# Two-layer trunk (S5 mixer, dilated attention, conv-GLU): the low part of the keys kept per head in both row halves, so that both products of a score tile use 128 rows

## The chip, the cores and the metric

One core of one Trainium2 chip runs the whole program. The metric is the device time of the program in microseconds (us), the median of its runs. The engines are TensorE (PE, with its weight loads as PEld), VectorE (DVE), ScalarE (ACT), GpSimd (POOL) and SyncE (SP), which issues nearly all DMAs.

## The reference

A trunk of two layers over 1024 tokens of 1024 features, fp32. Layer 0 mixes with a state-space model (S5), layer 1 with attention; each is followed by a conv-GLU feed-forward, with layer norms around. Cut to the attention, in which the change lies:

```python
kv = h @ w_kv                                 # keys and values: 3 groups x 16 heads x 64
q = (h @ w_q) * 64 ** -0.5
for g, dil in ((0, 1), (1, 4), (2, 16)):      # nearest group, two dilated groups
    # residue blocks of 128 tokens with step dil; a block sees itself and the one before it
    s = einsum('brnqhe,brnkhe->brnhqk', qb, kb) + bias[g]      # scores, 64 features per head
    s = where(valid, s, -1e30)
    lse = logsumexp(s); p = exp(s - lse)
    o_g = einsum('brnhqk,brnkhe->brnqhe', p, vb)
w = softmax(stack(lse over the 3 groups))     # the groups merged by their weights
out = sum_g w_g * o_g  ->  @ w_out
```

## The kernel before, in words

**Precision.** A product of two fp32 matrices is made of parts: a tensor is split into a high part (rounded to fp32r) and a low part (the rest, in fp32r). `mm3` (L86 to L90) gives three products: high x high, high x low, low x high.

**Stages.** S5 (to about 205 us), its gate and output projection, the first feed-forward, values of all heads (`value_tile`, to DRAM as `vscr`), then from about 1400 to 2440 us the attention by pairs of heads, then its output projection and the second feed-forward. The products outside the attention are not touched.

**A pair of heads** (`Pair`, eight pairs). For each of three groups `proj` (L407) makes queries and keys of both heads, 128 features x 1024 tokens: per tensor two halves of 512 tokens, each 24 products (tile qk, L88 to L90). ScalarE brings a half from PSUM to tile qt (L430 for queries, L432 for keys) and writes its high part (L436); for keys it writes it a second time (L438). GpSimd subtracts to get the low part (L441).

The layout decides which products can be made. X is one tile per head (named qs in the profile, for queries and keys alike), 128 rows: head 0 has its 64 features in rows 0 to 63, head 1 in rows 64 to 127. Queries: the high part in the head's own 64 rows, the low part in the other 64. Keys: the high part in both halves. The low part of the keys stands in kl, one tile for both heads, each head in its own 64 rows.

A score tile takes two products into the same PSUM region (`smm`, L481): L488 over 128 rows (query high and low, by key high in both halves) and L489 over the head's 64 rows (query high by key low). Their weights are the queries (128 columns); the keys move, 256 or 128 columns. Score tiles: per head 7 of 256 and 1 of 128 columns in the nearest group, 4 and 4 in each dilated group, so 384 in all, 240 of 256 columns and 144 of 128. Two or four of them share a PSUM buffer (tile s, four buffers, shared with the transposes).

VectorE adds the bias and takes the maximum in one instruction per score tile (L477), into p. ScalarE makes the exponentials (L508, L534). `softmax` (L540) merges the statistics and scales p (L557, L564) on VectorE. `output` (L584) loads V of the three groups (L589, tile V, three buffers), transposes p on TensorE (tile t, L605), brings it to SBUF (L608) and multiplies with V (tile o, L615); first the nearest group, then both dilated ones into a second PSUM tile.

**What orders the work.** A scheduler puts each engine's instructions into a fixed order at build time; an engine then runs its list in order and waits where an operand or a buffer isn't there. Projections run about a group ahead of scores: the queries and keys of the next group or the next pair are made between the scores of this one, and serve to fill TensorE's time during the softmax. Buffers bound how far: pool `ap` (`setup`, L669) has eight buffers for q (X and kl, five to a group), two for qt, three for V. So the last tiles of a group's keys wait until the scores of the group before have read theirs. SP has one queue: a load that waits for a buffer holds up those behind it.

Of the kernel before, what the change touches and what calls it, by code (L numbers as in the profile page):

```python
# [9 lines left out]
F32 = mybir.dt.float32  # L10
F32R = mybir.dt.float32r
# [7 lines left out]
P = 128  # L19
# [9 lines left out]
class Pool:  # L29
    """a tile pool with a fixed number of buffers for every tag"""  # L30
# [9 lines left out]
class Net:  # L40
# [55 lines left out]
    def type1(self, ps, w, xT, halves=(0, 1)):  # L96
        """ps[P, 1024] = w^T x, w = (hi, lo) as [P, KT, 128]"""
# [39 lines left out]
    def ln_final(self, acc, gb, tt):  # L137
        """with gain and bias: ((x - mean) gain) r + bias"""
# [21 lines left out]
    def to_T(self, accs, hf, li, xp, tmp):  # L160
        """transposes four normalized token tiles; gain and bias; split. -> list of KT tiles"""
# [20 lines left out]
    def ffn(self, l, accs, hT, xp, wd_pool, first_half, after):  # L182
        """first_half(): called when the products that need only the first half of hT are out"""
# [71 lines left out]
        for i in range(nch):  # L255
            c = list(range(i * CH, i * CH + CH))
            aT = [up(f) for f in c]
            if i == nch - 1:
                # the transposed input is no longer needed: its buffers take the last weights
# [10 lines left out]
def bias_onehot():  # L270
    """[64, 3, 384] selectors: row b picks rel_bias[b], row 32 the mask; column j is distance 255 - j"""
# [24 lines left out]
def attn_bias_rows(net, pool, ps1):  # L296
    """rel_bias by distance, one row for each head -> DRAM"""
# [16 lines left out]
def attn_bias(net):  # L314
    """a copy of the rows for each query row, to be read skewed"""
# [7 lines left out]
def skew(scr, h0, q0, qstep, nq):  # L323
    """[nq, 2 heads, 256] view: element (q, k) = row[127 - q + k], q = q0 + qstep * i"""
# [5 lines left out]
def tok_cols(xh, g, j):  # L330
    """columns of key tile j of layout g in a token half tile [P, 512]"""
    if g == 0:
        q = (j % 4) * P
        return slice(q, q + P)
    return slice(j // 2, 512, 4)
# [6 lines left out]
def value_tile(net, blk, j, hT, ws, ps, st):  # L342
    """values of four heads for a key tile: token-major, per group in its key order, kept in DRAM"""
# [12 lines left out]
def values_first(net, hT, pool):  # L356
    """the value tiles that need only the first half of the tokens, before the second half is there"""
# [9 lines left out]
def attention(net, hT, ap, ws):  # L367
# [25 lines left out]
    # the buffers of hT take the output  # L393
# [13 lines left out]
def proj(net, w, hT, g, isq, ap):  # L407
# [3 lines left out]
    # per head, rows of 64: queries (hi, lo), keys (hi, hi); the second head has its halves swapped  # L411
    X = [ap.tile([P, T], F32R, "q", "qs") for _ in range(2)]
    kl = None if isq else ap.tile([P, T], F32R, "q", "kl")
    for hf in range(2):
# [18 lines left out]
        for h in range(2):  # L433
# [5 lines left out]
            lo = X[h][o, sl] if isq else kl[r, sl]  # L439
# [997 lines left out]
```

## Time and profile before

| | us |
|---|---|
| runs | 3305.84, 3303.48, 3299.15 |
| median | 3303.48 |
| span of the profiled execution, first to last instruction | 3296.0 |
| around the span, taken as median less span | 7.5 |
| TensorE busy | 3128.0 (95%) |
| VectorE busy | 1745.0 (53%) |
| ScalarE busy | 1072.5 (33%) |
| GpSimd busy | 589.8 (18%) |
| mean granted clock of TensorE, share of full | 0.952 |

The device time of the profiled execution itself isn't given beside its span, so the span is set against the median of the runs. How to read the rows: a timeline row has start, duration, engine, line, operation, tiles as out<-in, operand shape and count; in brackets the idle time ahead of it and what ended it. Matmuls are pipelined, so the duration of one is longer than what it keeps the engine from the next; the step from start to start shows that. In a row of grouped instructions stand count, busy time, mean ns of one, idle time ahead. PEclk is the share of full clock that TensorE was granted.

### The profile page before, as it was taken

The page shows a single profiled execution, that of the slowest core. Times are in us where ns is not written, and L with a number is a line of the kernel's source. Part 1 is how long each engine was busy: PE and PEld are TensorE (multiplying, and loading weights), DVE is VectorE, ACT ScalarE, POOL GpSimd, SP SyncE. Part 2 cuts the span into 40 slices and gives each one's busy share as a digit, 9 for nine tenths or more (in the row PEclk, how much of TensorE's full clock was granted, in tenths as well). Part 3 has the DMA queues.
Part 4 walks back from the last instruction along what each step waited for, and adds up shares of the span by engine and source line. Part 5 has one row for each costly group of instructions (what it writes and reads, how often), then busy time and mean ns, then how long its engine had stood idle before and what let it go on. Part 6 is the DMA issues. An engine that isn't in the chain of part 4 may idle for free.

```text
span 3296.0 us, 36786 instructions
## 1 busy us (share of the span) xinstructions
PE 3128.0 (95%) x14422; PEld 2524.8 (77%) x14422; DVE 1745.0 (53%) x3348; ACT 1072.5 (33%) x1868; POOL 589.8 (18%) x447
## 2 busy tenths in 40 slices
PE   4789999999999999999999999999969999999997
PEld 3668878888888789977767777777747788888886
DVE  8954764455444621135455455355457755454447
ACT  2433332222222311145444445454433322222222
POOL 8910140000000000022222222222343500000001
PEclk8889999999999999999989998998979999999999
DMA  5232321111111243211111111111134111111121
GB/s 172 65 117 77 122 64 45 52 52 45 45 52 50 92 125 99 90 36 48 55 51 43 43 58 37 51 61 36 52 127 135 64 52 43 54 50 47 45 64 51
DMA packets 98413, 219.63 MB, mean 67 GB/s; under 512 B 9664, under 2 KB 51248, under 8 KB 98240
## 3 DMA queue, kind: packets, MB, share of 16 engines
q1 hardware_dynamic: 96128, 207.85, 19.9%
q0 software_dynamic: 2112, 9.44, 0.9%
q8 instruction: 113, 1.85, 0.2%
q14 instruction: 60, 0.49, 0.0%
HBM read 191.49 MB, written 35.20 MB: 69 GB/s over the span
## 4 chain that ended last, share of the span: by engine, by line
PE 84%; DVE 8%; POOL 4%; ACT 2%; issue 1%; DMA 1%; SPq 0%; ACTq 0%; POOLq 0%; DVEq 0%
PE dn L236 14%; PE up L89 10%; PE up L88 10%; PE up L90 10%; PE qk L88 5%; PE qk L90 4%; PE qk L89 4%; PE s L489 4%; PE s L488 3%; PE v L88 3%; PE v L90 3%; PE v L89 3%; PE o L615 2%; DVE p L564 2%; PE t L605 2%; PE wo L88 2%
## 5 line engine op out<-in xcount | busy, mean ns | idle before, releaser
L84 DVE TENSOR_TENSOR wl<-raw,wh 128x1024 fp32r<-128x1024 f32 x261 | 337.6, 1295 | 739.0 <-ACT wh L83 738.4
L83 ACT CAST wh<-raw 128x1024 fp32r<-128x1024 f32 x261 | 274.0, 1051 | 1104.0 <-PE up L89 473.2
L88 PE MATMUL up<-hT,wh 128*128 128x512 f32 x1408 | 549.4, 391 | 12.1 <-DVE u L212 12.1
L89 PE MATMUL up<-hT,wh 128*128 128x512 f32 x1408 | 549.6, 391 | 1.0 <-DVE hT L84 1.0
L90 PE MATMUL up<-hT,wl 128*128 128x512 f32 x1408 | 549.3, 391 | 0.0
L441 POOL TENSOR_TENSOR qs<-qt,qs 64x512 fp32r<-64x512 f32 x96 | 125.8, 1311 | 1290.6 <-ACT qs L436 1246.6
L88 PE MATMUL qk<-hT,wh 128*128 128x512 f32 x768 | 328.6, 428 | 0.0
L89 PE MATMUL qk<-hT,wh 128*128 128x512 f32 x768 | 322.7, 420 | 0.0
L90 PE MATMUL qk<-hT,wl 128*128 128x512 f32 x768 | 322.6, 420 | 0.0
L88 PEld LDWEIGHTS up<-hT,wh 128*128 128x128 f32 x1408 | 265.3, 189 | 67.7 <-issue 12.9
L89 PEld LDWEIGHTS up<-hT,wh 128*128 128x128 f32 x1408 | 265.6, 189 | 57.4 <-DVE hT L84 2.3
L90 PEld LDWEIGHTS up<-hT,wl 128*128 128x128 f32 x1408 | 265.5, 189 | 55.2
L212 DVE SCALAR_TENSOR_TENSOR u<-up,cw,u 128x1022 f32<-128x1022 f32 (+1 forms) x176 | 224.6, 1278 | 30.4 <-ACT u L208 28.2
L477 DVE CUSTOM_DVE_ANT_0 p<-s,bt 128x256 f32<-128x256 f32 (+1 forms) x384 | 125.6, 372 | 211.8 <-PE s L489 211.1
L246 DVE TENSOR_TENSOR acc<-acc,dn 128x1024 f32<-128x1024 f32 x144 | 174.9, 1217 | 92.1 <-PE dn L236 90.0
L236 PE MATMUL dn<-wh,ah 128*128 128x512 f32 x704 | 216.8, 389 | 0.0
L236 PE MATMUL dn<-wl,ah 128*128 128x512 f32 x704 | 216.7, 389 | 0.0
L236 PE MATMUL dn<-wh,al 128*128 128x512 f32 x704 | 216.6, 389 | 0.0
L441 POOL TENSOR_TENSOR kl<-qt,qs 64x512 fp32r<-64x512 f32 x96 | 123.6, 1293 | 391.5 <-PE s L488 261.3
L88 PEld LDWEIGHTS qk<-hT,wh 128*128 128x128 f32 x768 | 156.2, 203 | 38.8 <-issue 4.7
L90 PEld LDWEIGHTS qk<-hT,wl 128*128 128x128 f32 x768 | 156.4, 204 | 34.5
L89 PEld LDWEIGHTS qk<-hT,wh 128*128 128x128 f32 x768 | 156.7, 204 | 32.9 <-issue 0.7
(248 smaller groups left out, 5096.6 us busy)
## 6 DMA issues: line engine op xcount, KB each, us to landing
raw<-in_w_up SPq DMA_DIRECT2D x88, 512.0 KB, 3.5
raw<-in_w_out SPq DMA_DIRECT2D x48, 512.0 KB, 3.5
raw<-in_w_down SPq DMA_DIRECT2D x44, 512.0 KB, 3.5
raw<-in_w_v SPq DMA_DIRECT2D x25, 512.0 KB, 3.5
vscr<-vs SPq DMA_DIRECT2D x48, 256.0 KB, 2.3
V<-vscr SPq DMA_DIRECT2D x24, 512.0 KB, 4.1
raw<-in_w_q SPq DMA_DIRECT2D x24, 512.0 KB, 3.5
raw<-in_w_k SPq DMA_DIRECT2D x24, 512.0 KB, 3.6
```

What stands on the lines that cost most here:

```text
L83: nc.scalar.copy(hi, x)
L84: (eng or nc.vector).tensor_tensor(out=lo, in0=x, in1=hi.bitcast(F32), op=ALU.subtract)
L88: nc.tensor.matmul(out, lh, rh, start=first, stop=False)
L89: nc.tensor.matmul(out, lh, rl, start=False, stop=False)
L90: nc.tensor.matmul(out, ll, rh, start=False, stop=last)
L212: nc.vector.scalar_tensor_tensor(out=tf[:, d:], in0=ps[:, : T - d], scalar=cw[:, d, ft : ft + 1], in1=tf[:, d:], op0=ALU.mult, op1=ALU.add,)
L236: nc.tensor.matmul(ps[:, h * 512 : h * 512 + 512], l_, w[wi][:, h * 512 : h * 512 + 512], start=(i == 0 and l_ is ah and wi == 0), stop=(i ...
L246: nc.vector.tensor_tensor(out=accs[tt][:], in0=accs[tt][:], in1=ps[:], op=ALU.add)
L441: e.tensor_tensor(out=lo, in0=tmp[r], in1=hi.bitcast(F32), op=ALU.subtract)
L477: nc.vector.tensor_tensor_reduce(out=out, in0=s, in1=b, scale=1.0, scalar=-3.0e38, op0=ALU.add, op1=ALU.max, accum_out=m)
L488: nc.tensor.matmul(out, qx[:, qs], kv[0], start=True, stop=False)
L489: nc.tensor.matmul(out, qx[r, qs], kv[1], start=False, stop=True)
```

## The change

The low part of the keys, kl, becomes one tile per head like X, and GpSimd writes it into both halves of the 128 rows: twice the operations for kl. The second product of a score tile then takes all 128 rows of the queries (high and low) by key low in both halves; that adds the product low x low, which was left out. Both products stand on one line now. Of the attention's buffers q gets nine instead of eight (six tiles to a group now), V two instead of three. In the changed file comments and docstrings are gone, and lines from here on have numbers one or two smaller (L440 for L441, L488 for both L488 and L489, L588 for L589).

```diff
@@ proj
     X = [ap.tile([P, T], F32R, "q", "qs") for _ in range(2)]
-    kl = None if isq else ap.tile([P, T], F32R, "q", "kl")
+    kl = None if isq else [ap.tile([P, T], F32R, "q", "kl") for _ in range(2)]
...
             if not isq:
                 nc.scalar.copy(X[h][o, sl], tmp[r])
-            lo = X[h][o, sl] if isq else kl[r, sl]
-            e = nc.gpsimd
-            e.tensor_tensor(out=lo, in0=tmp[r], in1=hi.bitcast(F32), op=ALU.subtract)
+            for lo in [X[h][o, sl]] if isq else [kl[h][r, sl], kl[h][o, sl]]:
+                nc.gpsimd.tensor_tensor(out=lo, in0=tmp[r], in1=hi.bitcast(F32), op=ALU.subtract)
@@ smm
-            r = slice(64 * h, 64 * h + 64)
-            qx, kx, kl = q[0][h], k[0][h], k[1]
+            qx, kv = q[0][h], [k[0][h][:], k[1][h][:]]
             if isinstance(ks, int):
-                kv = [x.rearrange("p (n r q) -> p n r q", n=2, r=4)[:, :, ks, :] for x in (kx[:], kl[r])]
+                kv = [x.rearrange("p (n r q) -> p n r q", n=2, r=4)[:, :, ks, :] for x in kv]
             else:
-                kv = [kx[:, ks], kl[r, ks]]
-            nc.tensor.matmul(out, qx[:, qs], kv[0], start=True, stop=False)
-            nc.tensor.matmul(out, qx[r, qs], kv[1], start=False, stop=True)
+                kv = [x[:, ks] for x in kv]
+            for i in range(2):
+                nc.tensor.matmul(out, qx[:, qs], kv[i], start=(i == 0), stop=(i == 1))
@@ setup
-    return net.pool("ap", ctx, q=8, qt=2, V=3, oT=1, p1=2, p4=2, bt=1, pt=4)
+    return net.pool("ap", ctx, q=9, qt=2, V=2, oT=1, p1=2, p4=2, bt=1, pt=4)
```

The scheduler makes a new order from this. TensorE, in the second pair, at the first score tile of head 1 in the nearest group (s is the score tile, qs the keys' and the queries' X, kl the low part of the keys, qk a projection). Before, the products alternate between lines and rows, and after one tile projections follow:

```order
L488 MATMUL s_10271<-qs_9780,qs_9710 128x128
L489 MATMUL s_10271<-kl_9781,qs_9710 128x128
L488 MATMUL s_10271<-qs_9780,qs_9710 128x256
L489 MATMUL s_10271<-kl_9781,qs_9710 128x256
L88 MATMUL qk_10516<-hT_7472,wh_10510 128x512
L89 MATMUL qk_10516<-hT_7472,wh_10510 128x512
L90 MATMUL qk_10516<-hT_7472,wl_10511 128x512
```

The same place of TensorE's list afterwards:

```order
L88 MATMUL qk_10572<-hT_7656,wh_10535 128x512
L89 MATMUL qk_10572<-hT_7656,wh_10535 128x512
L488 MATMUL s_10291<-qs_9795,qs_9725 128x128
L488 MATMUL s_10291<-kl_9797,qs_9725 128x128
L488 MATMUL s_10291<-qs_9795,qs_9725 128x256
L488 MATMUL s_10291<-kl_9797,qs_9725 128x256
L488 MATMUL s_10298<-qs_9795,qs_9725 128x256
L488 MATMUL s_10298<-kl_9797,qs_9725 128x256
```

The tile stood ahead of 20 projection products and stands behind 21 of them now, with the three other tiles of its head right after it. GpSimd, at the keys of the second group of the same pair (kl, qt and qs as above). Before:

```order
L441 TENSOR_TENSOR kl_10387<-qt_10413,qs_10385 64x512
L441 TENSOR_TENSOR kl_10387<-qt_10446,qs_10385 64x512
L441 TENSOR_TENSOR kl_10387<-qt_10413,qs_10386 64x512
L441 TENSOR_TENSOR kl_10387<-qt_10446,qs_10386 64x512
L441 TENSOR_TENSOR qs_10514<-qt_10541,qs_10514 64x512
L441 TENSOR_TENSOR qs_10515<-qt_10541,qs_10515 64x512
```

The same place of GpSimd's list afterwards:

```order
L440 TENSOR_TENSOR kl_10407<-qt_10434,qs_10405 64x512 x2
L440 TENSOR_TENSOR kl_10407<-qt_10469,qs_10405 64x512 x2
L440 TENSOR_TENSOR kl_10408<-qt_10434,qs_10406 64x512 x2
L440 TENSOR_TENSOR kl_10408<-qt_10469,qs_10406 64x512 x2
L440 TENSOR_TENSOR qs_10539<-qt_10566,qs_10539 64x512
L440 TENSOR_TENSOR qs_10540<-qt_10566,qs_10540 64x512
```

The order is the same, both halves of head 0 first, with every kl operation doubled and the queries' low parts behind eight operations instead of four. SP, at the end of the first pair's output (V is a V load, raw a weight load, oscr the store of the output). Before, all three loads there are for the second pair:

```order
L589 DMA V_10859<-vscr 128x1024
L75 DMA raw_11320<-in_w_q 128x1024
L589 DMA V_10861<-vscr 128x1024
L589 DMA V_10863<-vscr 128x1024
L666 DMA oscr<-oT_10105 128x1024
```

The same place of SP's list afterwards:

```order
L588 DMA V_9872<-vscr 128x1024
L75 DMA raw_11355<-in_w_q 128x1024
L588 DMA V_10894<-vscr 128x1024
L588 DMA V_10896<-vscr 128x1024
L665 DMA oscr<-oT_10125 128x1024
```

The first load there is now the first pair's own third one, which the products of its last group read soon after; the second pair's third load has moved to the same place a pair later.

## Prediction

> **What bounds the kernel now.** I read the page first (busy shares, then the chain that ended last), then TensorE's timeline in the attention stage, then windows for the granted clock.
>
> ```profile
> span 3296.0 us, 36786 instructions
> ...
> PE 3128.0 (95%) x14422; PEld 2524.8 (77%) x14422; DVE 1745.0 (53%) x3348; ACT 1072.5 (33%) x1868; POOL 589.8 (18%) x447
> ...
> PE 84%; DVE 8%; POOL 4%; ACT 2%; issue 1%; DMA 1%; SPq 0%; ACTq 0%; POOLq 0%; DVEq 0%
> PE dn L236 14%; PE up L89 10%; PE up L88 10%; PE up L90 10%; PE qk L88 5%; PE qk L90 4%; PE qk L89 4%; PE s L489 4%; PE s L488 3%; PE v L88 3%; PE v L90 3%; PE v L89 3%; PE o L615 2%; DVE p L564 2%; PE t L605 2%; PE wo L88 2%
> ```
>
> TensorE (PE; PEld is its weight load) is busy in 95% of the span and carries 84% of the chain, the score products (tile s) 7%; DVE comes next with 53% busy. So a microsecond saved on PE counts, as long as no wait takes its place. The change works in the attention stage, about 1400 to 2400 us, on the two products that make a score tile: L488 over 128 rows, L489 over 64. Two stretches of PE's timeline (start, duration, ...):
>
> ```profile
> 1700.51 0.38 PE L488 MATMUL s<-qs,qs 128*128 128x256 f32 x1
> 1700.82 0.38 PE L489 MATMUL s<-kl,qs 64*128 64x256 f32 x1
> 1701.13 0.39 PE L488 MATMUL s<-qs,qs 128*128 128x256 f32 x1
> ...
> 1716.38 0.32 PE L489 MATMUL s<-kl,qs 64*128 64x128 f32 x1
> 1716.64 0.33 PE L488 MATMUL s<-qs,qs 128*128 128x128 f32 x1
> 1716.90 0.32 PE L489 MATMUL s<-kl,qs 64*128 64x128 f32 x1
> ```
>
> Products overlap, so the cost of one is the step from its start to the next start: 0.31 us with 256 columns, 0.26 with 128. Halving the columns saves only 0.05; about 0.2 us of each step does not depend on them. Compare stretches in which the rows do not change:
>
> ```profile
> 1755.48 0.39 PE L88 MATMUL qk<-hT,wh 128*128 128x512 f32 x1
> 1755.71 0.39 PE L89 MATMUL qk<-hT,wh 128*128 128x512 f32 x1
> ...
> 1756.16 0.46 PE L488 MATMUL s<-qs,qs 128*128 128x256 f32 x3
> 1756.55 0.38 PE L489 MATMUL s<-kl,qs 64*128 64x128 f32 x2
> ...
> 1554.01 1.53 PE L605 MATMUL t<-ident,p 128*128 128x128 f32 x12
> 1555.29 0.48 PE L88 MATMUL qk<-hT,wh 128*128 128x512 f32 x1
> ```
>
> A projection product of 512 columns steps at 0.23, less than an L489 of 256. Three L488 that the order happens to put in a row take 0.39 to the next start, 0.13 each, the change to 64 rows at their end included. Twelve transposes, each 128x128 with weights of its own, take 1.28, so 0.107 each. The 0.2 us is the price of the change between 128 and 64 rows, paid at every score product.
>
> **The change part by part.**
>
> (1) The score products. Counts, by form:
>
> ```profile
> L489 PE MATMUL s<-kl,qs 64*128 64x256 f32 x240 | 96.3, 412 | 0.0
> ...
> L488 PE MATMUL s<-qs,qs 128*128 128x256 f32 x240 | 92.9, 394 | 0.7 <-DVE mg L477 0.5 <-ACT qs L438 0.2
> ...
> L489 PE MATMUL s<-kl,qs 64*128 64x128 f32 x144 | 52.6, 365 | 0.0
> L488 PE MATMUL s<-qs,qs 128*128 128x128 f32 x144 | 48.8, 339 | 0.0
> ```
>
> At full clock they cost 480 x 0.31 + 288 x 0.26 = 224 us today. Afterwards all 768 use 128 rows. For 256 columns I take 0.12 (the row of three, less the change at its end), for 128 columns 0.11 (the transposes): 480 x 0.12 + 288 x 0.11 = 89 us. Gain 135. Bounds: no gain if the 0.2 us belongs to something else; 224 - 768 x 0.107 = 142 if every step falls to the transposes'.
>
> The weight load of one product:
>
> ```profile
> 1755.48 0.19 PEld L89 LDWEIGHTS qk<-hT,wh 128*128 128x128 f32 x1
> ```
>
> It runs beside the product ahead of it (0.39 long, step 0.23), and all rows there are in use. The Trainium skill ("TensorE: Matmul & The Clock Gate", Part 3, The mechanism) says otherwise: a weight load overlaps a running product only where the row groups differ. By that rule the change would put every load behind its product; the row speaks against it, and rival B prices it.
>
> (2) The granted clock. One window over the stage, then four of 4 us from one pair (busy times by engine, then PEclk, DMA share, GB/s):
>
> ```profile
> 1400.00:2400.00 1000.00, 980.59 (x4335) 722.04 (x4333) 510.21 (x1875) 473.85 (x1066) 261.92 (x202) 0.91 0.15 48
> ...
> 1552.00:1556.00 4.00, 4.00 (x37) 3.40 (x36) 1.12 (x2) 2.47 (x3) 0.00 (x0) 1.00 0.22 70
> ...
> 1576.00:1580.00 4.00, 4.00 (x17) 2.37 (x14) 2.77 (x9) 0.00 (x0) 0.00 (x0) 1.00 0.70 206
> 1580.00:1584.00 4.00, 4.00 (x11) 2.94 (x11) 1.81 (x9) 3.72 (x9) 3.91 (x4) 0.62 0.52 187
> ...
> 1592.00:1596.00 4.00, 4.00 (x10) 3.00 (x11) 3.78 (x17) 0.20 (x1) 2.23 (x2) 0.50 0.01 2
> ```
>
> 0.91 over 1000 us is 90 us lost. The clock falls to half right behind runs of scores, although PE counts as busy in all of the 4 us: with a step of 0.31, of which half a 512-column step (0.11) is work, the array is two thirds empty. Afterwards a run of 16 such products lasts 1.9 us instead of 5, nearly filled, with projections around it. I take three quarters of the 90 back, 68 us; bounds 0 and 90. The Trainium skill (same page, Part 1) has the gate at half or full rate by activity in windows of about 3.4 us; whether it counts these short products as activity no row here shows, which is rival C.
>
> (3) GpSimd (POOL). Each key tensor's low part is now written twice per half and head, 8 operations instead of 4.
>
> ```profile
> 1580.02 5.09 POOL L441 TENSOR_TENSOR kl<-qt,qs 64x512 fp32r<-64x512 f32 x4 [37.22 <-PE s L488]
> ...
> L441 POOL TENSOR_TENSOR kl<-qt,qs 64x512 fp32r<-64x512 f32 x96 | 123.6, 1293 | 391.5 <-PE s L488 261.3 <-issue 62.3 <-ACT qs L436 58.9
> ...
> L441 POOL TENSOR_TENSOR qs<-qt,qs x96: 1258/1277/1552, 1410.7 to 2371.4; 64x512 fp32r<-64x512 f32 x96
> ```
>
> That is 96 x 1.29 = 124 us more, on an engine with 262 of these 1000 us busy. It costs time only where PE waits. The tightest place: the keys of the next group wait for head 0's last score (the row at 1580.02), then take 8 x 1.29 = 10.3 us instead of 5.1. In the new order PE has between that score and the next group's first second product 31 projection products (7.1 us) and 16 scores (1.9): 9.0 us, and needs the first two operations only (2.6 us). Head 1's keys, ready after 10.3, are asked for 3 to 5 us later still. The query parts queued behind on POOL (5.2 us) are asked for after some 26 us. No cost; if POOL were late by all eight, 1.3 us a group, 31 us in all.
>
> (4) VectorE's (DVE's) reductions free the four PSUM buffers of the scores.
>
> ```profile
> 1578.94 0.42 DVE L477 CUSTOM_DVE_ANT_0 p<-s,bt 128x256 f32<-128x256 f32 x1 [0.48 <-PE s L489]
> ...
> 1579.29 0.42 DVE L477 CUSTOM_DVE_ANT_0 p<-s,bt 128x256 f32<-128x256 f32 x1
> ...
> 1595.09 0.28 DVE L477 CUSTOM_DVE_ANT_0 p<-s,bt 128x128 f32<-128x128 f32 x1
> ...
> 1595.30 0.28 DVE L477 CUSTOM_DVE_ANT_0 p<-s,bt 128x128 f32<-128x128 f32 x1
> ```
>
> Steps of 0.35 and 0.21, against 0.24 and 0.22 for PE's two products afterwards: PE, which DVE now waits for, gets ahead inside a run, by 0.9 us over eight tiles of 256, and projections stand between the runs. Then the softmax. Behind the last score PE has 101 projection products (22.9 us) before transposes that DVE must release; it had 103 before, and waited already:
>
> ```profile
> 1537.26 2.60 PE L605 MATMUL t<-ident,p 128*128 128x128 f32 x16 [0.83 <-DVE p L557]
> ```
>
> This wait grows by the two products (0.5) and by DVE's lag behind the last scores (about 1). With 1 to 2 us inside the runs I count 4 us a pair, 32 us for eight pairs; bounds 0 and 80, ten a pair: 3 more if no projection covers what DVE is slower by over a pair's 48 reductions (30 x 0.35 + 18 x 0.21 = 14, PE 11), and 3 more if the softmax wait grows by as much.
>
> (5) Two V buffers instead of three. The third load now waits for the nearest group's last product and then has to land before the last group's first product.
>
> ```profile
> V<-vscr SPq DMA_DIRECT2D x24, 512.0 KB, 4.1
> ...
> 1554.11 0.33 SPq L589 DMA_DIRECT2D V<-vscr  x1
> ```
>
> A load was issued at this very place before, 1554.11, right where the transposes of the row at 1554.01 begin. In the new order PE has from there about 5.8 us: 21 transposes and 13 projections (2.2 + 3.0) and the first products of the other dilated group (0.6). The load lands after 4.1. Behind it on SP stand only the next query weights, wanted a group later. I count 5 us, most of it in the last pair, where no projection fills in; bounds 0 and 8 x 4.1 = 33. The q pool's ninth buffer keeps the old waits: 6 tiles a group in 9, as 5 in 8, leaves three free.
>
> Sum: 135 + 68 - 32 - 5 = 166 us. The profiled execution's span is 3296.0; the median, 3303.48, has 7.5 us around it. 3296 - 166 + 7.5 = 3137.5: I say 3138.
>
> **The rivals.**
>
> B, the loads stand exposed (the page's rule): each of the 768 steps is then a load, 0.19, which saves 224 - 146 = 78; the runs stay half empty, half the clock (34) returns, less 37: 75 us, 3229. For it: no row has a long series of short 128-row products in fp32r. Against it: three of them in 0.39, and projections stepping at 0.23 with a load of 0.19 each.
>
> C, the clock stays where it is: 135 - 37 = 98 us, 3206. For it: runs of 128-column scores fill half of their step, and waits of PE may count as idle. Against it: no half clock stands in the stretches of transposes and projections around 1554 (1.00 there), which are just as short.
>
> D, slower: GpSimd becomes the bound of the score half of a pair. There it has 8 + 4 + 8 + 4 operations, 31 us at 1.29, beside PE's 41 (119 projections 27, scores 11, the rest 3). It decides from 1.7 us an operation on. At 2.5 us it takes 60, 19 more than PE, 152 us over eight pairs; each wait drops the clock, so the 68 are not won, and the old 90 double: 152 + 90 + 37 - 135 = 144 slower, 3447; at 2.1 still 3370. For it: two operations now read and write the same rows back to back. Against it: the longest POOL operation of this form took 1.55 us, the median 1.28.
>
> That the products still change rows is ruled out by the order: every score row is L488 with both operands of 128 rows. A remainder is that nothing moves because the softmax chain ends last whatever PE does; its 26 us a pair are covered by projections that remain, so I give it little.
>
> **How the numbers follow.** Forecast 0.63, B 0.08, C 0.13, D 0.05, no change 0.02, and 0.09 for more than forecast (all bounds good: 142 + 90 = 232, 3071). The forecast's own range is 3100 to 3180 by the bounds of (2) and (4). To leave out no more than 0.2, the range reaches up over C to 3215 and stays at 3095 below. About 0.2% is what a measurement of this kernel can tell: the three runs lie 0.2% apart. Faster by more than that 0.93, within 0.02, slower 0.05.
>
> **What would show it.** Right: score steps of 0.12 and 0.11 in the timeline; the chain's score lines from 7% together to under 3%; a granted clock over 0.96 in the stage; kl at x192 on POOL with waits of PE for it near nothing; pairs some 20 us shorter. Wrong in (1): steps of 0.19 or more. Wrong in (2): 0.5 behind scores as before. Wrong in (3) to (5): PE idle for over 60 us of its busy stretch in the stage, against 1000 - 981 = 19 today.

## The result, and the profile after

Over four runs on one chip the changed kernel takes 3180.1 us (median; 3179.5 to 3185.7) against 3302.1 for the kernel before: a ratio of 0.9634, 95% interval 0.9621 to 0.9648. That is 122 us gained where 166 were forecast. The profiled execution went from a span of 3296.0 to 3183.7, so 112 us; single executions differ, and the one profiled after is the slowest of its four (3185.67, 2.0 us around its span), while the one profiled before would, with as much around its span, come to 3298, below its four (3299.15 to 3305.84). First its page: span, busy time by engine, the chain that ended last by engine and by line.

```profile
span 3183.7 us, 36883 instructions
...
PE 2963.2 (93%) x14422; PEld 2457.5 (77%) x14422; DVE 1809.4 (57%) x3348; ACT 1074.7 (34%) x1868; POOL 721.9 (23%) x543
...
PE 78%; DVE 11%; POOL 5%; ACT 3%; DMA 1%; issue 1%; SPq 0%; ACTq 0%; POOLq 0%; DVEq 0%
PE dn L236 15%; PE up L89 10%; PE up L88 10%; PE up L90 10%; PE qk L88 3%; PE qk L89 3%; PE qk L90 3%; PE v L88 3%; DVE p L556 3%; PE v L89 3%; PE v L90 3%; PE o L614 3%; ACT p L533 2%; PE t L604 2%; PE s L488 2%; DVE p L563 2%
```

The score products went from 7% of the chain to 2%. DVE's share rose from 8% to 11%, with a line that was not on the list before: the scaling of p with the first factor (L556; L557 in the kernel before). Now the score products in TensorE's timeline (start, duration of one; products overlap, so the step from start to start counts).

```profile
1561.43 0.28 PE L488 MATMUL s<-qs,qs 128*128 128x256 f32 x1
1561.55 0.28 PE L488 MATMUL s<-kl,qs 128*128 128x256 f32 x1
1561.67 0.28 PE L488 MATMUL s<-qs,qs 128*128 128x256 f32 x1
...
1592.30 0.28 PE L488 MATMUL s<-qs,qs 128*128 128x128 f32 x1
1592.41 0.27 PE L488 MATMUL s<-kl,qs 128*128 128x128 f32 x1
1592.52 0.27 PE L488 MATMUL s<-qs,qs 128*128 128x128 f32 x1
```

Steps of 0.12 and 0.11, as forecast. What did not come is seen in the whole attention stage. I cut it from the first score product to the last output product, the kernel before first, the changed one second (length, busy time of PE, PEld, DVE, ACT and POOL, then the granted clock).

```profile
1426.00:2444.00 1018.00, 980.46 (x4391) 717.85 (x4391) 538.79 (x1966) 484.11 (x1099) 270.19 (x208) 0.90 0.15 48
```

```profile
1427.00:2332.00 905.00, 810.99 (x4396) 645.11 (x4396) 601.88 (x1966) 486.44 (x1099) 401.99 (x303) 0.93 0.18 55
```

All of the 112 us lie here, within a microsecond: 1018 - 905 = 113. Each row splits into three: idle time of PE (length less busy), time lost to the clock (length times one less the clock, good to 5 us, since the clock has two digits), and the rest, which is PE's work at full clock. Before: 38 idle, 102 lost, 878 work. After: 94 idle, 63 lost, 748 work. The work fell by 130, the clock gave 39 back, and the idle time grew by 56: 130 + 39 - 56 = 113.

The idle time has a place. Two groups of TensorE, then one of GpSimd and three of VectorE (busy time, mean ns of one, then idle time just before them and its releaser), and last what the score products wait for in the stage (us in total, times, the longest).

```profile
L604 PE MATMUL t<-ident,p 128*128 128x128 f32 x624 | 105.3, 316 | 64.7 <-DVE p L556 64.7
L614 PE MATMUL o<-pt,V 128*64 128x256 f32 (+1 forms) x800 | 97.6, 349 | 4.3 <-DVE pt L607 3.1 <-ACT pt L607 0.7 <-DMA V<-vscr 0.4
...
L440 POOL TENSOR_TENSOR kl<-qt,qs 64x512 fp32r<-64x512 f32 x192 | 255.8, 1332 | 253.9 <-PE s L488 218.8 <-ACT qs L436 21.6 <-issue 2.2
...
L551 DVE COPY x<-st 32x4 f32<-32x4 f32 x256 | 103.5, 404 | 5.0 <-ACT p L507 1.2
L556 DVE TENSOR_SCALAR p<-p,e 128x256 f32<-128x256 f32 x112 | 92.7, 891 | 0.0
L476 DVE CUSTOM_DVE_ANT_0 p<-s,bt 128x256 f32<-128x256 f32 x240 | 89.7, 421 | 10.6 <-PE s L488 9.4
...
PE s L488 <- DVE st L476: 16.4, 14, 1.5
```

The same rows of the kernel before, for the groups that were not shown there:

```profile
L605 PE MATMUL t<-ident,p 128*128 128x128 f32 x624 | 95.4, 289 | 23.5 <-DVE p L557 23.5
...
L552 DVE COPY x<-st 32x4 f32<-32x4 f32 x256 | 63.5, 248 | 26.5 <-ACT p L508 22.5
L564 DVE TENSOR_SCALAR p<-p,e 128x512 f32<-128x512 f32 x60 | 44.5, 741 | 0.0
L564 DVE TENSOR_SCALAR p<-p,e 128x256 f32<-128x256 f32 x60 | 43.8, 729 | 0.2
L557 DVE TENSOR_SCALAR p<-p,e 128x256 f32<-128x256 f32 x112 | 39.6, 423 | 0.0
L477 DVE CUSTOM_DVE_ANT_0 p<-s,bt 128x256 f32<-128x256 f32 x240 | 92.7, 422 | 146.0 <-PE s L489 145.4
```

The transposes' wait for the scaling grew from 23.5 to 64.7 us. One long wait of it stands in the last pair of either kernel, 16.7 us before and 15.5 after; new are 5.5 us in each of the seven other pairs. And the scaling with the first factor, the same instruction on the same data, went from 423 to 891 ns, while the reductions beside it stayed at 421 and the scaling with the second factor (L564) did not grow (746 and 598 ns in the changed kernel). No row calls that a wait: the idle time before L556 is 0.0. The time stands inside the duration. The timeline of one pair shows with what it goes: VectorE's scalings, then GpSimd, then TensorE (a row of x8 is a run; the tile size in it is that of its first operation, and of the eight with the first factor seven are 128x256).

```profile
1612.66 8.62 DVE L556 TENSOR_SCALAR p<-p,e 128x128 f32<-128x128 f32 x8
1623.40 6.91 DVE L563 TENSOR_SCALAR p<-p,e 128x256 f32<-128x256 f32 x8
1632.46 0.81 DVE L556 TENSOR_SCALAR p<-p,e 128x128 f32<-128x128 f32 x3
1633.30 3.44 DVE L556 TENSOR_SCALAR p<-p,e 128x256 f32<-128x256 f32 x5
1636.84 2.73 DVE L563 TENSOR_SCALAR p<-p,e 128x256 f32<-128x256 f32 x8
```

```profile
1612.97 2.73 POOL L440 TENSOR_TENSOR qs<-qt,qs 64x512 fp32r<-64x512 f32 x2 [12.19 <-ACT qs L436]
1615.78 5.35 POOL L440 TENSOR_TENSOR kl<-qt,qs 64x512 fp32r<-64x512 f32 x4
1623.70 5.67 POOL L440 TENSOR_TENSOR kl<-qt,qs 64x512 fp32r<-64x512 f32 x4 [2.57 <-ACT qs L436]
1633.41 2.65 POOL L440 TENSOR_TENSOR qs<-qt,qs 64x512 fp32r<-64x512 f32 x2 [4.04 <-issue]
```

```profile
1626.91 0.39 PE L90 MATMUL qk<-hT,wl 128*128 128x512 f32 x1
1632.80 1.97 PE L604 MATMUL t<-ident,p 128*128 128x128 f32 x8 [5.50 <-DVE p L556]
...
1639.20 0.63 PE L88 MATMUL qk<-hT,wh 128*128 128x512 f32 x1
1639.62 0.63 PE L89 MATMUL qk<-hT,wh 128*128 128x512 f32 x1
```

Eight scalings from 1612.66 take 8.62 us, 1.08 each, beside GpSimd's six operations (1612.97 to 1621.13). Three at 1632.46, with GpSimd idle, take 0.81, so 0.27 each; the five behind them, beside the two operations of GpSimd that run from 1633.41 to 1636.06, take 3.44. The eight of the second factor take 6.91 beside four operations of GpSimd and 2.73 with none. Head 1's scalings come behind all that, TensorE has run out of projections by then and stands still for 5.50 us, and the projections behind the wait step at 0.43 instead of 0.23: the clock is at half.

**Theory L:** in the changed kernel VectorE's scaling waits for GpSimd's operations, one by one, and the twice as many subtractions on GpSimd are what the missing time pays for. **Rival R:** VectorE is late only because the scores are finished sooner, and GpSimd doesn't matter. The Trainium skill (SBUF — State Buffer, Who interferes with whom) has a rule for L: VectorE's copies and scalings in SBUF can run in a mode that takes a pair of ports shared with GpSimd, and whichever of the two is issued first holds it for its whole instruction. The rows so far agree for VectorE, in one of the two groups of copies of the statistics too (248 to 404 ns; the other went from 194 to 175).

### The profile page after: what moved, and what is told of

It is laid out like the page before. It is cut to its first block, busy times and chain, and to the rows that moved or that the text cites. A ratio compares the mean times of both kernels' runs of the same rounds, so it can differ in the third digit from the quotient of the medians.

```text
span 3183.7 us, 36883 instructions
## 1 busy us (share of the span) xinstructions
PE 2963.2 (93%) x14422; PEld 2457.5 (77%) x14422; DVE 1809.4 (57%) x3348; ACT 1074.7 (34%) x1868; POOL 721.9 (23%) x543
## 4 chain that ended last, share of the span: by engine, by line
PE 78%; DVE 11%; POOL 5%; ACT 3%; DMA 1%; issue 1%; SPq 0%; ACTq 0%; POOLq 0%; DVEq 0%
PE dn L236 15%; PE up L89 10%; PE up L88 10%; PE up L90 10%; PE qk L88 3%; PE qk L89 3%; PE qk L90 3%; PE v L88 3%; DVE p L556 3%; PE v L89 3%; PE v L90 3%; PE o L614 3%; ACT p L533 2%; PE t L604 2%; PE s L488 2%; DVE p L563 2%
## 5 line engine op out<-in xcount | busy, mean ns | idle before, releaser
L88 PE MATMUL up<-hT,wh 128*128 128x512 f32 x1408 | 548.7, 391 | 12.1 <-DVE u L212 12.1
L440 POOL TENSOR_TENSOR qs<-qt,qs 64x512 fp32r<-64x512 f32 x96 | 127.4, 1327 | 1174.7 <-ACT qs L436 1140.9
L440 POOL TENSOR_TENSOR kl<-qt,qs 64x512 fp32r<-64x512 f32 x192 | 255.8, 1332 | 253.9 <-PE s L488 218.8
L88 PE MATMUL qk<-hT,wh 128*128 128x512 f32 x768 | 310.6, 404 | 0.0
L90 PE MATMUL qk<-hT,wl 128*128 128x512 f32 x768 | 306.8, 399 | 0.0
L89 PE MATMUL qk<-hT,wh 128*128 128x512 f32 x768 | 306.4, 399 | 0.0
L88 PEld LDWEIGHTS qk<-hT,wh 128*128 128x128 f32 x768 | 148.8, 194 | 30.2 <-issue 2.7
L89 PEld LDWEIGHTS qk<-hT,wh 128*128 128x128 f32 x768 | 148.1, 193 | 29.1
L90 PEld LDWEIGHTS qk<-hT,wl 128*128 128x128 f32 x768 | 147.4, 192 | 29.5
L604 PE MATMUL t<-ident,p 128*128 128x128 f32 x624 | 105.3, 316 | 64.7 <-DVE p L556 64.7
```

The costliest lines, as they stand in the source:

```text
L88: nc.tensor.matmul(out, lh, rh, start=first, stop=False)
L89: nc.tensor.matmul(out, lh, rl, start=False, stop=False)
L90: nc.tensor.matmul(out, ll, rh, start=False, stop=last)
L440: nc.gpsimd.tensor_tensor(out=lo, in0=tmp[r], in1=hi.bitcast(F32), op=ALU.subtract)
L604: nc.tensor.transpose(ps[:, i * P : i * P + P], b, net.ident[:])
```

## The experiments

All times are medians beside runs of the kernel before on the same chip (3297 to 3301); ratios are to it, with their 95% interval. The kernel's scheduler places the instructions anew for each variant, so the order moves each time. In the runs on the buffers below, a change that adds no operation moves the time by 13 to 49 us together with its new order. So the time of a run is not the price of its edit alone, and the argument rests first on the durations of the operations and on the waits.

### GpSimd's second operation taken away: the copy on ScalarE

```diff
+            lo = X[h][o, sl] if isq else kl[h][r, sl]
+            nc.gpsimd.tensor_tensor(out=lo, in0=tmp[r], in1=hi.bitcast(F32), op=ALU.subtract)
+            if not isq:
+                nc.scalar.copy(kl[h][o, sl], lo)
```

> The changed kernel, but the second copy of the keys' low part is a copy on ScalarE instead of a second subtraction on GpSimd: GpSimd's work in the attention is that of the kernel before, ScalarE gets 96 copies of about 0.6 us (57 us in 1000). Theory L (in the changed kernel VectorE's scaling of p waits for GpSimd's operations, one by one): the scaling with the first factor, 423 ns before and 891 ns in the changed kernel, falls to 420-600 ns; the transposes' wait for it (64.7 us) falls to 25-45 us; the time falls from 3180 to about 3150 (3135-3165). Rival R (VectorE was simply late since the scores are finished sooner, and GpSimd doesn't matter): the scaling stays near 890 ns, the wait stays near 65 us, the time stays at 3175-3185, or rises by up to 15 where the copies on ScalarE delay the exponentials.

Measured: 3116.1 us, ratio 0.9435 (0.9419 to 0.9451). The two groups of the wait:

```profile
L606 PE MATMUL t<-ident,p 128*128 128x128 f32 x624 | 93.8, 287 | 36.4 <-DVE p L558 35.8
...
L558 DVE TENSOR_SCALAR p<-p,e 128x256 f32<-128x256 f32 x112 | 54.1, 551 | 0.0
```

L holds, R falls: scaling from 891 to 551 ns, wait from 64.7 to 35.8 (17.2 of it in the last pair), and 64 us less in spite of 58.7 us of copies added to ScalarE. That is twice the 30 expected and below the range given, and the stage's row tells why:

```profile
1428.00:2261.00 833.00, 776.24 (x4399) 624.03 (x4397) 544.56 (x1966) 539.38 (x1193) 270.64 (x208) 0.98 0.19 60
```

57 us idle, 37 less than in the changed kernel, and only 17 lost to the clock, 46 less. Here no wait of a steady pair is longer than about 1 us, since the projections also fall between the first transposes in this kernel's order; part of the gain is therefore that order's, and I do not put all 64 us down to GpSimd.

### GpSimd's second operation added to the kernel before

```diff
-            e = nc.gpsimd
-            e.tensor_tensor(out=lo, in0=tmp[r], in1=hi.bitcast(F32), op=ALU.subtract)
+            for _ in range(1 if isq else 2):
+                nc.gpsimd.tensor_tensor(out=lo, in0=tmp[r], in1=hi.bitcast(F32), op=ALU.subtract)
```

> The kernel before, in which GpSimd makes each low part of the keys twice into the same place: GpSimd's work of the changed kernel under the products of the kernel before. Theory L: the scaling goes from 423 ns to 600-900 ns, the transposes' wait for it from 23.5 us to 40-65 us, and the time rises by 15 to 45 us over 3302, to 3317-3347. Rival R: GpSimd's second operation is hidden, the scaling stays near 420 ns, the time stays at 3299-3306.

Measured: 3336.1 us, ratio 1.0105 (1.0086 to 1.0123): 35 us slower, with TensorE's products unchanged.

```profile
L557 DVE TENSOR_SCALAR p<-p,e 128x256 f32<-128x256 f32 x112 | 77.2, 754 | 0.0
...
L605 PE MATMUL t<-ident,p 128*128 128x128 f32 x624 | 106.2, 305 | 62.5 <-DVE p L557 62.4
```

The scaling goes to 754 ns and the wait to 62.4 us, without a single score product being faster. By R neither should have moved, so R is refuted by this run alone. How much of the 35 us is the new order's is not separated.

### The second product on 64 rows again

```diff
-            for i in range(2):
-                nc.tensor.matmul(out, qx[:, qs], kv[i], start=(i == 0), stop=(i == 1))
+            r = slice(64 * h, 64 * h + 64)
+            nc.tensor.matmul(out, qx[:, qs], kv[0], start=True, stop=False)
+            nc.tensor.matmul(out, qx[r, qs], kv[1][r], start=False, stop=True)
```

> The changed kernel with the second product of a score tile on the 64 rows of its head again, as before; the second copy of the low part is still made, and not used. Score steps go back to 0.31 us (256 columns) and 0.26 us (128). If the 128 rows themselves give the gain: score products back to about 224 us from 110, the granted clock in the pairs' stage back to 0.91, the time at 3300-3340, the upper end where theory L holds (GpSimd's doubled work slows VectorE's scaling to 600-900 ns here too), the lower end where rival R holds (scaling near 420 ns). If the change gained by something else (buffers, order), the time stays under 3250.

Measured: 3347.5 us, ratio 1.0142 (1.0123 to 1.0161), slightly above what was expected. The 128 rows themselves are worth 3347 - 3180 = 167 us; all else that the change brings costs 46 (3347 - 3301), where the run above, with GpSimd's added operations alone, has 35. The first factor's scaling is at 557 ns, short of the 600 to 900 that L expected, but the second factor's went up instead, to 872 and 843 ns for 128x512 and 128x256 (741 and 729 in the kernel before), and the transposes' wait is 52.2 us.

### The scaling in another form

The scaling also writes the sum of its result, into a tile that nothing reads. GpSimd's operations, twice as many, stay. The scaling with the second factor is changed in the same way.

```diff
-            nc.vector.tensor_scalar(out=x, in0=x, scalar1=f1[:, n : n + 1], scalar2=None, op0=ALU.mult)
+            j = sp.tile([P, 1], F32, "acj", "acj")
+            nc.vector.tensor_scalar(out=x, in0=x, scalar1=f1[:, n : n + 1], scalar2=0.0, op0=ALU.mult, op1=ALU.add, accum_out=j[:])
```

> The changed kernel with the scaling of p on VectorE in the form that also writes its sum (into a tile that nothing reads). Theory L says that the usual form waits for GpSimd and not that VectorE has too much to do. The Trainium skill, SBUF — State Buffer, Who interferes with whom, counts the usual form among those that take the pair of ports shared with GpSimd, and not this one. Theory L: an operation of 128x256 takes one and the same time beside GpSimd and alone, 350-450 ns as the 128x256 reduction's 421 ns, in place of 270 alone and about 1070 beside GpSimd; mean of the first factor's scaling from 891 to 350-450 ns; the transposes' wait from 64.7 to 25-45 us; time 3145-3165. Rival R: the scaling's wait isn't for GpSimd's ports; the mean stays at 800 ns or more, the time at 3175-3195.

Measured: 3140.0 us, ratio 0.951 (0.9497 to 0.9524).

```profile
L609 PE MATMUL t<-ident,p 128*128 128x128 f32 x624 | 97.4, 288 | 25.5 <-DVE p L557 24.8 <-ACT pt L612 0.3
...
L557 DVE TENSOR_SCALAR_CACHE_REDUCE p<-p,e 128x256 f32<-128x256 f32 x112 | 47.8, 467 | 0.0
...
1621.23 2.50 PE L609 MATMUL t<-ident,p 128*128 128x128 f32 x12 [0.64 <-DVE p L557]
...
L488 PE MATMUL s<-kl,qs 128*128 128x256 f32 x240 | 61.5, 302 | 15.1 <-POOL kl L440 15.1
```

The form is slower by itself (467 ns on the mean, against 361 for the usual form in the kernel below in which GpSimd is idle) and yet halves the group, since it does not wait. Sorted by whether an operation of GpSimd overlaps them, its operations of 128x256 take 468 ns (133 that are overlapped) and 472 ns (39 that are not) in the median; those of the usual form in the changed kernel take 1384 ns (91) and 347 ns (81). The time falls by 40 us, 5 us further than expected, and the wait of 5.50 us, behind the same run of projections as in the changed kernel, is 0.64. So the cause is not how much VectorE has to do but, as L says, something that the usual form shares with GpSimd and this one does not. One cost is new: the score products wait 21.9 us for the keys' low part (7.1 in the changed kernel), up to 1.9 us at a time.

### Both at once

> The copy of the low part on ScalarE and the scaling in the form that writes its sum, together. Theory L: the two act on the same wait (64.7 us in the changed kernel, 36 with the copy on ScalarE, 25 with the other form), so their gains of 64 and 40 us don't add up; the scaling of 128x256 at 380-470 ns whatever GpSimd does, the transposes' wait 10-25 us, time 3085-3110. Rival: what is left of the wait is VectorE's own work, and the copy on ScalarE gains by the score products' wait for GpSimd: time 3112-3120, as with the copy alone.

Measured: 3137.8 us, ratio 0.9513 (0.9497 to 0.9529), slower than the copy on ScalarE alone and outside the ranges of both sides. The scaling is at 472 ns and the wait for it at 25.5, at the upper edge of what L expected. But the slower form gives back what the waiting took: all scalings of p together keep VectorE busy for 128 us here and for 125 with the copy alone (178 in the changed kernel). And 13.8 us of idling stand before the first and 12.1 before the second products of the score tiles, most of it for VectorE's reductions and for ScalarE's copies, where the copy alone had 2.4 and 8.9. So there was little left to gain and the remaining waits moved to another place; why this order brings more of them is not settled.

### GpSimd idle in the attention

The copy on ScalarE, the subtractions on VectorE. Left for GpSimd are 22 operations (30 us) in the last pair.

```diff
-            nc.gpsimd.tensor_tensor(out=lo, in0=tmp[r], in1=hi.bitcast(F32), op=ALU.subtract)
+            nc.vector.tensor_tensor(out=lo, in0=tmp[r], in1=hi.bitcast(F32), op=ALU.subtract)
```

> The copy of the low part on ScalarE, and the 192 subtractions on VectorE instead of GpSimd: GpSimd does nothing in the attention. Theory L: the usual form of the scaling falls to what it takes with GpSimd idle, 270-340 ns for 128x256 and 400-700 for 128x512, with no operation at 1 us; the small copies of the statistics fall from 290 to 160-200 ns; VectorE gets 192 subtractions of 0.5-0.9 us (96-173 us, in stretches where it waits for scores now): time 3085-3125. Rival R (VectorE's amount of work sets the wait, not GpSimd): the waits for VectorE grow with its added work, time over 3130.

Measured: 3101.2 us, ratio 0.9409 (0.9391 to 0.9427), the lowest median of all, 79 us below the changed kernel (74 by the ratios). Its interval overlaps that of the copy on ScalarE.

```profile
1423.00:2248.00 825.00, 784.96 (x4399) 629.92 (x4398) 566.57 (x2152) 540.51 (x1193) 29.58 (x22) 0.98 0.19 60
```

```profile
L558 DVE TENSOR_SCALAR p<-p,e 128x256 f32<-128x256 f32 x112 | 33.5, 361 | 0.0
...
L440 DVE TENSOR_TENSOR kl<-qt,qs 64x512 fp32r<-64x512 f32 x96 | 64.7, 681 | 14.3 <-ACT qs L436 12.5
...
L606 PE MATMUL t<-ident,p 128*128 128x128 f32 x624 | 88.1, 284 | 17.2 <-DVE p L558 17.2
```

VectorE does 131 us of subtractions more (64.7 here and 66.2 for the queries), and yet TensorE's wait for the scaling is the shortest of all kernels here: 17.2 us, 14.9 of it in the last pair. A subtraction takes 681 ns on VectorE and 1332 on GpSimd, and over the stage VectorE is busy for less time than in the changed kernel (567 against 602 us).

### What the price of a score step belongs to: the order of the products

The kernel before, every product with its own rows, but within a tile of PSUM first all products on 128 rows, then all on 64.

```diff
+        def run(ms):
+            for i in range(2):
+                for m in ms:
+                    m[i](start=(i == 0 and m is ms[0]), stop=(i == 1 and m is ms[-1]))
```

> The kernel before, its products unchanged in number and rows, but within each tile of PSUM all products on 128 rows come first and then all on 64 rows: 320 changes between the two in the eight pairs instead of 768. Theory S (the price of a score step is that of the change of rows): a product behind one of its own kind takes 0.12-0.15 us, one behind a change 0.26-0.31 us; of the 135 us between the score products of before and after, 79 go (448 of 768), and part of the 68 us of the clock with them: time 3185-3235 from 3302. Rival W (a product on 64 rows is dear by itself, or every product of a tile that has both kinds): the steps stay at 0.26-0.31 us in whatever order, time 3295-3310.

Measured: 3176.1 us, ratio 0.9624 (0.9599 to 0.9649): the whole gain of the change, without a second copy and without more work for GpSimd, and below the 3185 to 3235 that theory S expected. A stretch of its timeline (a row of x4 or x2 is a run of one kind), and its attention stage from the first score product to the last output product:

```profile
1597.34 0.67 PE L488 MATMUL s<-qs,qs 128*128 128x128 f32 x4
1597.93 0.66 PE L489 MATMUL s<-kl,qs 64*128 64x128 f32 x4
1598.52 0.50 PE L488 MATMUL s<-qs,qs 128*128 128x256 f32 x2
1598.95 0.50 PE L489 MATMUL s<-kl,qs 64*128 64x256 f32 x2
...
1424.00:2323.00 899.00, 860.71 (x4400) 662.35 (x4398) 532.16 (x1966) 485.48 (x1099) 274.27 (x208) 0.95 0.18 55
```

Eight products with 128 columns take 1.18 us here (1597.34 to 1598.52), 0.15 each, where they took 0.26 each in alternation; the 64-row products among them are no dearer than the others. With 256 columns two take 0.43. The price is that of the change, as the prediction had it, and theory S holds. The stage splits into 38 us idle, 45 lost to the clock and 816 of work: against the kernel before that is 62 of work (S expected 79), 57 of the clock and nothing of the waits. So that the two times are equal is in part chance: the changed kernel saves twice as much work (130) and loses it again to waits (56) and to the clock behind them. The run shows that as much could be had with no operation more.

### The buffers by themselves

The kernel before with nine and two buffers; the changed kernel with eight and three; the ordered one with nine and two; the one with GpSimd idle with eight and three.

```diff
-    return net.pool("ap", ctx, q=8, qt=2, V=3, oT=1, p1=2, p4=2, bt=1, pt=4)
+    return net.pool("ap", ctx, q=9, qt=2, V=2, oT=1, p1=2, p4=2, bt=1, pt=4)
```

> The kernel before with the buffers of the changed one alone: nine for the queries' and keys' tiles, two for the values'. The prediction gave this 5 us (0 to 33). The run with 64 rows in the changed layout stood 11 us above the kernel before with GpSimd's operations doubled; if that is the price of the buffers, the time is 3307-3318 here, with PE's waits for V near 5-10 us; if the buffers cost nothing (one more for the queries and keys makes up for it), 3297-3305.

> The changed kernel with the buffers of the kernel before (eight for the queries' and keys' tiles, three for the values'). The prediction said that two buffers for the values cost 5 us (0 to 33): then this is at 3147-3180. The kernel before gained 20 us from the changed buffers, though: where the ninth buffer for the queries and keys is what counts, this is above the changed kernel by 15 us or more, since it holds 8 buffers for 6 tiles a group instead of 9: 3195-3230.

> The kernel before with its score products ordered by rows within each tile of PSUM, and with nine and two buffers: no operation more than in the kernel before. If the gains of the two add up (122 and 20 us), 3145-3165, below the changed kernel without any of its second copies; if the buffers helped only by something that the order has removed already, 3170-3182.

> The kernel with the copy on ScalarE and the subtractions on VectorE (3101), with eight and three buffers instead of nine and two. The change of buffers gained 20 us in the kernel before and lost 13 us in the changed one. If three buffers for the values are what the 128-row products need, 3080-3095; if what the buffers do hangs on the order of the work that the scheduler makes of each kernel and the waits for GpSimd were what the 13 us stood on, 3095-3110; if nine buffers count for six tiles a group, over 3115.

Measured: 3280.1 us, ratio 0.994 (0.9922 to 0.9957), for the kernel before, so the new buffers gain 17 to 20 there, which neither expectation had. 3167.0, ratio 0.9592 (0.9573 to 0.9612), for the changed kernel with the old buffers, so there they cost 13. 3155.8, ratio 0.9565 (0.9542 to 0.9588), for the ordered one, 20 less. 3149.8, ratio 0.9543 (0.9523 to 0.9564), for the one with GpSimd idle and the old buffers, 49 more (44 by the ratios). Three in favour of nine and two, one against. Where the values have two buffers, TensorE's waits for their load come to 0.4 to 0.6 us in all (0.4 in the row of the output products above), so the mechanism that the prediction named, TensorE waiting for V, is not what decides. The two numbers of buffers were never changed apart, the order that the scheduler makes of each kernel differs, and which of the differences counts stays open.

### The cheap version without GpSimd

> The same, with the 192 subtractions of the low parts on VectorE: GpSimd does nothing in the attention and nothing is copied twice. Theory L: the scaling at 270-360 ns for 128x256, the transposes' wait under 20 us; against the kernel with 128 rows, the copy on ScalarE and the subtractions on VectorE (3101) it has some 30 us more of score products (141 against 112) and 58 us less on ScalarE: 3115-3140. Rival: VectorE's added work delays the reductions and with them the score products: over 3145.

Measured: 3153.9 us, ratio 0.9553 (0.9529 to 0.9577), no different from the one with GpSimd at work (3155.8), outside what L expected and where the rival had it. Yet the rival's reason isn't seen: no score product waits for a reduction. The scaling is at 365 ns and the wait at 18.3 us (16.2 in the last pair), about as L has it, but with one set of subtractions on GpSimd the wait was only 29.9 us. The stages, first with GpSimd at work, then without:

```profile
1432.00:2313.00 881.00, 845.73 (x4384) 652.54 (x4384) 525.74 (x1966) 484.18 (x1099) 274.90 (x208) 0.96 0.18 57
```

```profile
1423.00:2295.00 872.00, 848.07 (x4395) 660.25 (x4395) 563.95 (x2152) 486.80 (x1099) 30.12 (x22) 0.95 0.18 57
```

With GpSimd at work 35 us are idle and 35 lost to the clock; without it 24 and 44. So most of what the idle time gave back, the clock took; the work differs by 7 us, and the split is good to 5.

## Why the prediction was right, and where its sum was not

The sign, the main mechanism and the range hold; the sum was 44 us too large. The forecast's own range, 3100 to 3180, ends where the measured 3180.1 stands, but it does not follow from the bounds of (2) and (4), which give 3084 to 3254; the wider one holds because it was drawn up over rival C. Of the 166 forecast, the split of the stage shows 113 (122 by the medians): 5 less of work, 29 less of the clock, 19 more of waits than (4) and (5) had.

- **(1) The score steps**, forecast 135: right. The steps are 0.12 and 0.11, the work at full clock fell by 130, and the order experiment shows that the price is that of changing rows: 0.19 us with 256 columns and 0.15 with 128, where the prediction said 0.2. Rival B would have steps of 0.19; it is out.
- **(2) The clock**, forecast 68: 39, and 0.93 in the stage where over 0.96 was the sign. The scores no longer pull it down, but the new wait does: in the row at 1632.80 the clock is at half behind 5.50 us of idling. In the trace of the changed kernel it stands at half in the stage only there, about 10 us in each of seven pairs, and in the last pair. It comes back where that wait goes: 17 us are lost instead of 63 with the copy on ScalarE, all of them in the last pair. Rival C (no clock back) is out; the forecast had no term for a wait behind the scores.
- **(3) GpSimd**, forecast "No cost": this is the step that failed. The prediction asked only when the keys arrive, and on that it was nearly right (7.1 us of waits for them in all, but 21.9 once VectorE's wait is gone, in the run with the other form). It did not ask what else runs while GpSimd runs. The added 124 us of operations go with 35 us in the kernel before, where VectorE's scaling rises from 423 to 754 ns, and taking them off GpSimd with 64 in the changed kernel, some of it by the order. The rows for it stood in the profile of before: its scaling of 128x512 and of 128x256 with the second factor took 741 and 729 ns, nearly the same for half the elements, which fits a wait and not work; with GpSimd idle they take 493 and 352.
- **(4) VectorE**, forecast 32 at 4 us a pair: the waits for VectorE grew by 41 at the transposes and 17 at the scores, inside the bounds of 0 to 80 (with 7 more for the keys and 9 less at the output products that makes the 56 above). The 17 are the term that the prediction had as 1 to 2 us a pair inside the runs, 14 waits of up to 1.5 us for the reductions. The 41 are not for the reason given: at 1.5 us a pair they would be 12. The reductions kept their 421 ns; it was the scaling with the first factor that doubled.
- **(5) The buffers**, forecast 5: 13 us in the changed kernel, inside its bounds, and a gain of 17 to 20 in the kernel before. The load of V made TensorE wait once, for 0.4 us, so the mechanism that the step named is not what cost; what did stays open.

- **Rival D** had the right engine and the wrong mechanism: GpSimd did not become the bound, and its operations stayed at 1.33 us, far from the 1.7 from which it decides.

The prediction's own test of (3) to (5) was PE idle for over 60 us of its 1000 us stretch. There it is 100 (94 of them in the attention), and that test pointed at the right group of steps.

## What to carry to other kernels

Before work is moved to GpSimd, list what VectorE does beside it: its fp32 scalings and copies within SBUF waited here for GpSimd's fp32 operations, and the profile showed that as a longer duration, not as a wait. An operation whose mean duration doubles between two profiles, or that takes the same time for half the elements, may be waiting for something: look for what runs beside it. And before data are laid out twice so that products use the same rows, try to put products of one kind behind each other: here that alone gave the same gain.

## What the runs showed of the hardware

- VectorE's scalings of 128x256 in fp32 come every 0.27 us with GpSimd idle and every 1.08 beside GpSimd's 64x512 subtractions (1.33 us each); GpSimd's own operation went from 1293 to 1332 ns only. The form that also writes a sum takes 0.47 us in both cases, and the reduction that reads PSUM takes 0.42 in both (in the changed kernel 420 ns in the median for the 164 that an operation of GpSimd overlaps and for the 76 others).
- Operations with both inputs in SBUF can wait too, small as they are; the section of the Trainium skill named above says so of instructions that read two inputs there. In the last pair of the changed kernel GpSimd runs from 2291.99 to 2296.92; here are two VectorE operations of one form, one before the conflict and one in it:

```profile
2291.77 0.17 DVE L576 TENSOR_TENSOR t<-st,e 128x8 f32<-128x8 f32 x1
...
2293.31 1.18 DVE L571 TENSOR_TENSOR e<-st,M 128x8 f32<-128x8 f32 x1
```

- The change between 128 and 64 rows costs the same in either order. With 256 columns a step of 0.31 in alternation is 0.19 over the 0.12 without a change, and two products in 0.43 with one change are 0.19 over twice 0.12; with 128 columns it is 0.26 less 0.11, and 0.59 for four less 0.44, 0.15 both times.
- Behind a wait of TensorE of 3.8 us or more the clock was at half in each of the seven pairs before the last: 5.5 us in the changed kernel, with about 9 us at half behind it, 5.0 us in the one with 64 rows again, 3.8 us in the kernel before with GpSimd's operations doubled. Shorter waits went both ways: behind those of 1.9 us in the run with the other form of scaling it was at half for 6.8 us, behind those of 1.0 us in the ordered kernel for 3.4 us in five pairs of seven, and behind 1.5 us in the changed kernel and 1.0 us with the copy on ScalarE it stayed at 1.00. So the length of a wait alone does not settle it here, and what else does stays open.
